# VectorE's modulation slots are loaded at their own turn, and the condition rows are made behind each FFN's first up tile

## The chip, the cores and the metric

One core of one Trainium2 chip runs the whole program in one launch. The metric is the device time in microseconds, the median of several runs of the same kernel. TensorE is PE in the views, VectorE is DVE, ScalarE is ACT, GpSimd is POOL and SyncE is SP; SP issues the large loads.

## The reference, cut to what matters

Two transformer models are chained. The first has two layers (layers 0 and 1 of the kernel) over 512 latent tokens and 256 context tokens of width 1024; the second has one layer (layer 2). Every layer is modulated by a condition vector:

```python
def adaln(cond, w_mod, b_mod):
    m = jnp.dot(jax.nn.silu(cond), w_mod) + b_mod
    return jnp.split(m[..., None, :], 6, axis=-1)

sh1, sc1, g1, sh2, sc2, g2 = adaln(c, w_mod[l], b_mod[l])
h = modulate(rms_norm(x, norm1_g[l]), sh1, sc1)
...
x = x + g1 * jnp.einsum('blm,md->bld', mix, w_out[l])
x = x + g2 * swiglu(modulate(rms_norm(x, norm2_g[l]), sh2, sc2), w_ffn_in[l], w_ffn_out[l])
```

`w_mod` is 1024 x 6144 per layer, and it meets two condition vectors (latent and context), so it is a weight that is read once for two columns. `w_out` is 1024 x 1024, the FFN's hidden width is 2816. All of it is float32.

## The kernel before, in words

**Matmuls.** Each large product is made of three fp32r matmuls (`mm3`): high part by high part, high by low, low by high. Every weight therefore passes through a preparation: SP loads halves of 512 KB (128 x 1024) into the pool `raw`, which has four buffers; ScalarE casts quarters of 128 x 512 to `whi` (L242); GpSimd subtracts to get `wlo` (L244). The pool of `whi`/`wlo` holds two weights, so the cast of a weight waits until the matmuls of the one before the last are through.

**Two queues of loads.** The class `Weights` (L215 to L252) keeps a list of loads and gives them out in order. `next` (L248) issues whatever is missing up to one entry *ahead* of the one that it gives out. There are two such objects: `W` for the weights and `WM` for the modulation. A modulation *slot* is 256 columns of `w_mod`, 1 MB; it takes two `raw` buffers and holds them until its arithmetic is done. There are 72 slots, in the order of the list `MODS`, 24 for each layer. Both objects draw from the same four buffers and the same SP queue.

**Where slots are made.** The first 20 slots, and slots 48 and 49, are made by TensorE. The other 50 (`MODS_ROWS`: slots 20 to 47 in the FFN of layer 0, slots 50 to 71 in the FFN of layer 1) are made by VectorE in `mod_rows` (L357): four instructions of 128 x 1024 for each slot, two for each half and one condition vector each (L365, results `mjunk` or `raw`), and a small addition of the bias (L373, L377). They multiply by the *condition rows* `cr`: `cond_rows` (L348) loads them from DRAM on ScalarE's queue (L352) and passes them through two Silu of 128 x 1024 on ScalarE (L354). In the kernel before, `cond_rows` is called ahead of `ffn` in each of the layers 0 and 1.

**Order of the work.** The stages of a layer are: attention, pooling and convolution mixers; the out projection (`out_proj`), of which weight slots 2 and 3 of `w_out` come behind slots 0 and 1; the norm (`norm_mod`) of each half of 256 tokens as soon as that half of `xt` is through; then `ffn`, 22 up tiles of 128 gate and 128 up columns in groups, each group followed by its down projection. In layer 1 the out projection's last part has 8 tiles for each of two halves of the latent tokens; every tile ends in a `flush` on VectorE (L936, `xt` plus gated product), and the next tile but one into the same PSUM buffer waits for it. The norm squares `xt` on ScalarE (L437), sums partly on GpSimd (L441), makes the sums over partitions on TensorE (L449), scales them on VectorE (`rsv`, L310), takes the power on GpSimd (`rsy`, L311), transposes it to rows on TensorE (L336) and then makes `u` (L464), `hh` (L467) and `hl` (L470, L472).

In `ffn` each up tile j is 16 products of three matmuls with 512 columns into `s2t` (two buffers); then ScalarE's Silu of the gate half (L996), VectorE's product `sg` (L997), the split into `gh` and `gl`, and then `mod_fill(MODS_FFN[l][j])`, which makes so many slots there. `at[j]` is a hook that is called after tile j.

The program's order is not the final order on an engine: a list scheduler places each engine's instructions by its own estimate of when they are ready, within the dependencies and buffers. A small edit can therefore shift neighbours.

Of the kernel before, what the change touches and what calls it, by code (L numbers as in the profile page):

```python
# [24 lines left out]
NJ = FF // 128  # L25
# [91 lines left out]
MODS_ROWS = set(MODS[20:48] + MODS[50:72])  # L117
# [97 lines left out]
class Weights:  # L215


    def __init__(self, k, specs, ahead=1):
        self.k, self.specs, self.ahead = k, specs, ahead
        self.done, self.used, self.q = 0, 0, []  # L220

    def _load(self, spec):
        k, nc = self.k, self.k.nc
        kind, ap, n = spec
        hn = n // 2
        halves = (slice(0, hn), slice(hn, n))
        if kind == "mod":
            raws = []
            for s in halves:
                raw = k.p_raw.tile([128, hn], F32, tag="raw", name="raw")  # L230
                nc.sync.dma_start(out=raw, in_=ap[:, s])
                raws.append(raw)
            return raws
        p = k.p_w
        hi = p.tile([128, n], F32R, tag="whi", name="whi")
        lo = p.tile([128, n], F32R, tag="wlo", name="wlo")
        for s in halves:
            raw = k.p_raw.tile([128, hn], F32, tag="raw", name="raw")
            nc.sync.dma_start(out=raw, in_=ap[:, s])
            for q in (slice(0, hn // 2), slice(hn // 2, hn)):  # L240
                h = hi[:, s][:, q]
                nc.scalar.copy(out=h, in_=raw[:, q])  # L242
                eng = nc.vector if kind == "w2" and q.start else nc.gpsimd
                eng.tensor_tensor(out=lo[:, s][:, q], in0=raw[:, q], in1=h.bitcast(F32), op=ALU.subtract)  # L244
        return hi, lo

    def next(self, key):
        while self.done < min(len(self.specs), self.used + 1 + self.ahead):  # L248
            self.q.append(self._load(self.specs[self.done][1:]))
            self.done += 1  # L250
        assert self.specs[self.used][0] == key, (self.specs[self.used][0], key)
        self.used += 1  # L252
        return self.q.pop(0)


class K:
# [492 lines left out]


    MODS_MIX = [(4, 8, 0, 0), (0, 0, 2, 0)]
    MODS_FFN = [[2 if j % 4 == 1 else 1 for j in range(NJ)], [1] * NJ, [0] * NJ]

    LAST = [(0, 0, 0.2, 0.4, 0.6, 0.8, 1), (0, 0.1, 0.4, 0.7, 1)]
    SLOT = {"g": 0, "u": 1, "p": 2, "v0": 3, "q0": 4, "q1": 5, "v1": 6, "q2": 7, "q3": 8}
# [208 lines left out]
    def ffn(self, l, pf, hx, hc, xt, xc, then, at=None):  # L964
# [5 lines left out]
        for gi, (j0, jn, cn) in enumerate(DOWN[l]):  # L970
            gt = []
            for j in range(j0, j0 + jn):
# [28 lines left out]
                gt.append((gh, gl))  # L1001
                self.mod_fill(self.MODS_FFN[l][j], "ap", j == j0 + jn - 1)
                if at and j in at:
# [31 lines left out]
    def layer(self, l, then):  # L1035
# [8 lines left out]
        with self.pool(f"a{l}") as pa, self.pool(f"b{l}") as pb:  # L1044
# [4 lines left out]
            with self.pool(f"mix{l}") as pmix:  # L1049
# [79 lines left out]
                with self.urgent(0 if full else 500):  # L1129
                    run(win[0])  # L1130
                cur, k = -1, 0
                for hd in self.attn(pa, l, qk, v, mix, lambda g: splits(g, (3,))):
                    if hd != cur:
                        run(win[cur + 1][k:] if cur >= 0 else ())
                        self.flush_items((f"q{hd}", f"v{hd // 2}"))
                        if hd == 3:
                            hm, hmc = self.new_h("x"), (self.new_h("c") if full else None)
                        cur, k, t = hd, 0, 0
                    t += 1
                    n = int(len(win[hd + 1]) * share[hd + 1][t] + 0.01)  # L1140
                    run(win[hd + 1][k:n])
                    k = n
                    self.tick(4.0)
# [460 lines left out]
    def run(self):  # L1604
        nc, tc, I = self.nc, self.tc, self.I
# [22 lines left out]
        self.cond("c", "c_ctx")  # L1628
        self.W = Weights(self, self.plan())
        self.mods = list(MODS)  # L1630
        self.WM = Weights(self, [(("mod", l, s), "mod", I[f"w_mod{l}"][s], 2048) for l, s in self.mods])
        xs = [[p_dram.tile([128, KD * 256], F32, name=f"xs{l}{i}") for i in range(2)] for l in range(2)]
        v3 = lambda ap: ap.rearrange("p (k n) -> p k n", k=KD)

# [5 lines left out]
        def store_xt(dst, xt):  # L1640
            for i in range(2):
                (nc.sync, nc.scalar)[i].dma_start(out=v3(dst[i]), in_=xt[i])

        def norm_x(l, which, xt, dst, i):
            self.norm_mod(l, which, xt[i], 0, dst, G(i), i == 1)

        def norms(l, which, xt, dst, xc=None, dstc=None):

            def f(g):
                if g == 0:  # L1650
                    self.norm_mod(l, which, xc, 1, dstc)
                else:
                    norm_x(l, which, xt, dst, g - 1)
            return f
# [27 lines left out]
        xc, xt = self.x[0], self.x[1:]  # L1682
        with self.pool("u0") as self.p_u:
            h2c, h2 = self.new_h("c"), self.new_h("x")
            self.out_proj(0, self.out_weights(0, 2, 3), hm, hmc, xt, xc, norms(0, 2, xt, h2, xc, h2c))
            self.hc, self.hx = self.new_h("c"), self.new_h("x")
            with self.pool("f0", bufs=6) as pf:
                self.cond_rows(pf, 0)
                self.ffn(0, pf, h2, h2c, xt, xc, norms(1, 1, xt, self.hx, xc, self.hc))
            store_xt(xs[0], xt)  # L1690
        xpool.close()
        if self.stop == 0:
# [2 lines left out]
        xt = self.x[1:]  # L1695
        with self.pool("u1") as self.p_u:
            h2 = self.new_h("x")
            self.out_proj(1, self.out_weights(1, 2, 3), hm, None, xt, None, norms(1, 2, xt, h2))
            self.hc, self.hx = self.new_h("c"), self.new_h("x")
            with self.pool("f1", bufs=10) as pf:  # L1700
                self.cond_rows(pf, 1)
                xc2 = self.load_x(pf, "xc2", v3(I["c2T"]), NCX, 1)
                self.ffn(1, pf, h2, None, xt, None, norms(2, 1, xt, self.hx), {13: lambda: self.norm_mod(2, 1, xc2, 1, self.hc)})
            store_xt(xs[1], xt)
        xpool.close()
        if self.stop == 1:
# [6 lines left out]
        with self.pool("mix2") as pmix:  # L1713
            hm, xt = self.block2_mix(pmix, residual2)
        with self.pool("u2") as self.p_u:
            h2 = self.new_h("x")
# [87 lines left out]
```

## Time and profile before

| | |
|---|---|
| runs | 2583.49, 2572.78, 2583.26 us; median 2583.26 us |
| the profiled execution | 2590.84 us |
| its span, first to last instruction | 2589.0 us |
| mean granted TensorE clock | 0.964 of full speed |
| PE busy | 2424.3 us, 94% of the span |
| DVE, POOL, ACT busy | 1251.9, 1192.0, 887.6 us (48%, 46%, 34%) |
| mean DMA rate | 97 GB/s |

The profiled execution is 7.6 us above the median. PE's share is so high that only stretches in which it stands still, or runs at the low clock, can give time back; the layout in time matters: layer 0's out projection ends its first part near 424 us, layer 0's FFN fills 480 to 960 us, layer 1's out projection lies at 1310 to 1360 us, its FFN's first tiles at 1360 to 1390 us, and the FFN goes on to 1740 us.

### The profile page before, as it was taken

How to read it: one execution, taken by the hardware profiler on the slowest of the kernel's cores; microseconds unless marked ns; L12 is line 12 of the kernel's file. 1: busy time of each engine (PE TensorE's matmuls, PEld its weight loads, DVE VectorE, ACT ScalarE, POOL GpSimd, SP SyncE). 2: the span in 40 equal slices, each digit the busy share in tenths (PEclk: the TensorE clock that was granted, in tenths of full speed). 3: DMA queues.
4: the chain of work that ended last, by engine and by line, in shares of the span. 5: the costliest groups of instructions: out<-in, count | busy, mean ns of one | idle time of the engine just before them, and what ended most of it. 6: DMA issues, size and time to landing. Idle time of an engine off the chain costs nothing. (4 is left out here: it accounts for less than half of the span.)

```text
span 2589.0 us, 37145 instructions
## 1 busy us (share of the span) xinstructions
PE 2424.3 (94%) x14940; PEld 2121.5 (82%) x14940; DVE 1251.9 (48%) x2247; ACT 887.6 (34%) x1863; POOL 1192.0 (46%) x960
## 2 busy tenths in 40 slices
PE   7889979999999999988978999999998899999998
PEld 5878869988888889878778787888887788888887
DVE  4897464743533464497636455364322746210113
ACT  4334453312112124333534223224443543422222
POOL 3644323634334345555327656555222353555553
PEclk8889989999999999999989999999998899999999
DMA  7213312433423332211224544443111021233221
GB/s 244 63 50 111 121 69 66 139 113 107 139 90 130 106 125 82 68 34 37 94 82 135 166 147 155 141 144 100 39 37 47 17 98 50 82 97 97 95 94 57
DMA packets 69259, 250.53 MB, mean 97 GB/s; under 512 B 7520, under 2 KB 10848, under 8 KB 67168
## 3 DMA queue, kind: packets, MB, share of 16 engines
q1 hardware_dynamic: 65568, 232.29, 27.8%
q10 hardware_dynamic: 3520, 15.88, 1.6%
q8 instruction: 117, 1.92, 0.3%
q14 instruction: 54, 0.44, 0.1%
HBM read 241.85 MB, written 6.29 MB: 96 GB/s over the span
## 5 line engine op out<-in xcount | busy, mean ns | idle before, releaser
L244 POOL TENSOR_TENSOR wlo<-raw,whi 128x512 fp32r<-128x512 f32 x564 | 782.5, 1417 | 808.7 <-ACT whi L242 808.3
L242 ACT CAST whi<-raw 128x512 fp32r<-128x512 f32 x576 | 315.9, 616 | 784.6 <-PE s2t L271 378.6
L268 PE MATMUL s2t<-hh,whi 128*128 128x512 f32 (+1 forms) x1184 | 443.3, 376 | 3.6 <-DVE sg L997 3.6
L272 PE MATMUL s2t<-hh,wlo 128*128 128x512 f32 (+1 forms) x1184 | 443.9, 375 | 2.5 <-POOL wlo L244 2.5
L271 PE MATMUL s2t<-hl,whi 128*128 128x512 f32 (+1 forms) x1184 | 444.2, 376 | 1.1 <-POOL hl L470 1.1
L268 PE MATMUL pj<-hh,whi 128*128 128x256 f32 (+1 forms) x1088 | 337.2, 312 | 9.3 <-ACT hh L467 3.2
L271 PE MATMUL pj<-hl,whi 128*128 128x256 f32 (+1 forms) x1088 | 333.5, 307 | 2.1 <-POOL hl L470 1.1
L272 PE MATMUL pj<-hh,wlo 128*128 128x256 f32 (+1 forms) x1088 | 333.3, 308 | 0.0
L268 PEld LDWEIGHTS s2t<-hh,whi 128*128 128x128 f32 x1184 | 224.9, 191 | 45.2 <-DVE sg L997 5.9
L272 PEld LDWEIGHTS s2t<-hh,wlo 128*128 128x128 f32 x1184 | 225.6, 191 | 41.7 <-POOL wlo L244 2.9
L271 PEld LDWEIGHTS s2t<-hl,whi 128*128 128x128 f32 x1184 | 225.3, 190 | 41.1 <-POOL hl L470 1.9
L268 PEld LDWEIGHTS pj<-hh,whi 128*128 128x128 f32 x1088 | 212.8, 196 | 24.4 <-ACT hh L467 4.7
L365 DVE SCALAR_TENSOR_TENSOR mjunk<-raw,cr 128x1024 f32<-128x1024 f32 x100 | 140.3, 1403 | 178.9 <-DMA raw<-in_w_mod 166.4
L271 PEld LDWEIGHTS pj<-hl,whi 128*128 128x128 f32 x1088 | 212.0, 195 | 11.7 <-POOL hl L470 1.4
L272 PEld LDWEIGHTS pj<-hh,wlo 128*128 128x128 f32 x1088 | 212.2, 195 | 8.6 <-issue 1.3
L268 PE MATMUL pj<-whi,hh 128*128 128x256 f32 x672 | 197.3, 294 | 1.3 <-ACT v L741 0.9
L997 DVE TENSOR_TENSOR sg<-sg,s2t 128x512 f32<-128x512 f32 x66 | 45.0, 683 | 314.6 <-ACT sg L996 314.6
L271 PE MATMUL pj<-wlo,hh 128*128 128x256 f32 x672 | 196.2, 292 | 0.0
L272 PE MATMUL pj<-whi,hl 128*128 128x256 f32 x672 | 194.8, 290 | 0.0
L936 DVE SCALAR_TENSOR_TENSOR xt<-pj,mod,xt 128x256 f32<-128x256 f32 x224 | 101.7, 479 | 137.3 <-PE pj L272 137.0
L365 DVE SCALAR_TENSOR_TENSOR raw<-raw,cr 128x1024 f32<-128x1024 f32 x100 | 149.7, 1497 | 5.8
L271 PE MATMUL pj<-gl,whi 128*128 128x512 f32 (+1 forms) x400 | 144.2, 361 | 0.0
(392 smaller groups left out, 4644.0 us busy)
## 6 DMA issues: line engine op xcount, KB each, us to landing
raw<-in_w_mod SPq DMA_DIRECT2D x144, 512.0 KB, 4.2
raw<-in_w_up SPq DMA_DIRECT2D x132, 512.0 KB, 3.8
raw<-in_w_dn SPq DMA_DIRECT2D x66, 512.0 KB, 3.8
raw<-in_w_in SPq DMA_DIRECT2D x60, 512.0 KB, 3.9
raw<-in_w_out SPq DMA_DIRECT2D x24, 512.0 KB, 3.8
xt<-xs ACTq DMA_DIRECT2D x4, 1024.0 KB, 6.0
xt<-in_xT ACTq DMA_DIRECT2D x2, 1024.0 KB, 8.2
cr<-in_cr ACTq DMA_DIRECT2D x2, 1024.0 KB, 4.9
```

The lines of the kernel that those rows point to most:

```text
L242: nc.scalar.copy(out=h, in_=raw[:, q])
L244: eng.tensor_tensor(out=lo[:, s][:, q], in0=raw[:, q], in1=h.bitcast(F32), op=ALU.subtract)
L268: i = mm(ps, lhsT=lh, rhs=rh, start=start, stop=False)
L271: mm(ps, lhsT=lh, rhs=rl, start=False, stop=False)
L272: return mm(ps, lhsT=ll, rhs=rh, start=False, stop=stop)
L365: nc.vector.scalar_tensor_tensor(out=raw[i] if ci else self.junk, in0=raw[i], scalar=1.0, in1=self.CR[:, ci], op0=ALU.mult, op1=ALU.mult, ...
L936: self.nc.vector.scalar_tensor_tensor(out=x, in0=ps, scalar=col, in1=x, op0=ALU.mult, op1=ALU.add)
L997: nc.vector.tensor_tensor(out=sg[:, c], in0=sg[:, c], in1=p[:, 1], op=ALU.mult)
```

## The change

The slots of `MODS_ROWS` get a kind of their own, "rows". `next` does not load such a slot ahead: only when it is the slot that is asked for. `cond_rows` is no longer called ahead of `ffn` but through the hook behind up tile 0. Since no slot can be made before the condition rows are there, the two tables of how many slots each tile makes start with 0; the slots of tile 0 are moved to later tiles. The number of slots stays 28 in layer 0 and 22 in layer 1, and no engine gets or loses an instruction.

```diff
-        if kind == "mod":
+        if kind in ("mod", "rows"):
...
     def next(self, key):
-        while self.done < min(len(self.specs), self.used + 1 + self.ahead):
+        while self.done < min(len(self.specs), self.used + 1 + self.ahead) and (self.done <= self.used or self.specs[self.done][1] != "rows"):
             self.q.append(self._load(self.specs[self.done][1:]))
...
-    MODS_FFN = [[2 if j % 4 == 1 else 1 for j in range(NJ)], [1] * NJ, [0] * NJ]
+    MODS_FFN = [[0, 2, 2, 1] + [2 if j in (5, 9, 13, 17, 20) else 1 for j in range(4, NJ)], [0, 2] + [1] * 20, [0] * NJ]
...
-        self.WM = Weights(self, [(("mod", l, s), "mod", I[f"w_mod{l}"][s], 2048) for l, s in self.mods])
+        self.WM = Weights(self, [(("mod", l, s), "rows" if (l, s) in MODS_ROWS else "mod", I[f"w_mod{l}"][s], 2048) for l, s in self.mods])
...
-                self.cond_rows(pf, 0)
-                self.ffn(0, pf, h2, h2c, xt, xc, norms(1, 1, xt, self.hx, xc, self.hc))
+                self.ffn(0, pf, h2, h2c, xt, xc, norms(1, 1, xt, self.hx, xc, self.hc), {0: lambda: self.cond_rows(pf, 0)})
...
-                self.cond_rows(pf, 1)
                 xc2 = self.load_x(pf, "xc2", v3(I["c2T"]), NCX, 1)
-                self.ffn(1, pf, h2, None, xt, None, norms(2, 1, xt, self.hx), {13: lambda: self.norm_mod(2, 1, xc2, 1, self.hc)})
+                self.ffn(1, pf, h2, None, xt, None, norms(2, 1, xt, self.hx), {0: lambda: self.cond_rows(pf, 1), 13: lambda: self.norm_mod(2, 1, xc2, 1, self.hc)})
```

The lines of the changed kernel are one higher from L216 on. What the scheduler makes of it is read from the order of each engine's instructions. First SP, the loads of layer 1's out projection and of the FFN's first up tiles (`w_out` x2 is half of a pair of weight slots, `w_mod` x2 one modulation slot); before:

```order
L239 DMA raw<-in_w_out 128x1024 x2
L231 DMA raw<-in_w_mod 128x1024 x4
L239 DMA raw<-in_w_out 128x1024 x6
L239 DMA raw<-in_w_up 128x1024 x4
L231 DMA raw<-in_w_mod 128x1024 x2
L239 DMA raw<-in_w_up 128x1024 x2
L231 DMA raw<-in_w_mod 128x1024 x2
```

and now:

```order
L240 DMA raw<-in_w_out 128x1024 x2
L232 DMA raw<-in_w_mod 128x1024 x2
L240 DMA raw<-in_w_out 128x1024 x6
L240 DMA raw<-in_w_up 128x1024 x6
L232 DMA raw<-in_w_mod 128x1024 x4
L240 DMA raw<-in_w_up 128x1024 x2
```

One slot's two loads have moved from ahead of the last six loads of `w_out` to behind the third up tile's weight; from the fourth row on the two kinds take turns as before.

Second ScalarE in the same out projection, from the casts of the last `w_out` slots to the norm's squares (`s<-xt`; `mix` and `hh` belong to the attention's last head, `xc` is a load for layer 2); before:

```order
L242 CAST whi<-raw 128x512 x4
L910 ACTIVATE mix_9866<-ap,gs_94 128x256
L340 CAST hh<-mix_9866 128x256
L352 DMA cr<-in_cr 128x2048
L1601 DMA xc_13318<-in_c2T 128x2048
L242 CAST whi<-raw 128x512 x2
L354 ACT_TABLE_LOAD
L354 ACTIVATE cr<-cr 128x1024 x2
L242 CAST whi<-raw 128x512 x2
L437 ACTIVATE s<-xt_12392 128x256 x8
```

and now:

```order
L243 CAST whi<-raw 128x512 x8
L911 ACTIVATE mix_9866<-ap,gs_94 128x256
L341 CAST hh<-mix_9866 128x256
L1602 DMA xc_13309<-in_c2T 128x2048
L353 DMA cr<-in_cr 128x2048
L438 ACTIVATE s<-xt_12388 128x256 x6
L355 ACT_TABLE_LOAD
L355 ACTIVATE cr<-cr 128x1024 x2
L438 ACTIVATE s<-xt_12388 128x256 x2
```

The eight casts stand in one piece, and the table load and the two Silu have moved from between the casts to between the squares. On VectorE the five instructions of the slot (L365 x4, L373) that stood ahead of this out projection's first flush are gone from there. In layer 0 the Silu keep their place ahead of the casts.

Third VectorE at the norm of the second half ahead of layer 1's FFN; before:

```order
L472 SCALAR_TENSOR_TENSOR hl<-u,mod_87,hh 128x256
L365 SCALAR_TENSOR_TENSOR mjunk,macc<-raw,cr 128x1024
L365 SCALAR_TENSOR_TENSOR raw,macc<-raw,cr 128x1024
L310 TENSOR_SCALAR rsv<-ap 128x1 x2
L365 SCALAR_TENSOR_TENSOR mjunk,macc<-raw,cr 128x1024
L472 SCALAR_TENSOR_TENSOR hl<-u,mod_87,hh 128x256
L365 SCALAR_TENSOR_TENSOR raw,macc<-raw,cr 128x1024
L373 TENSOR_TENSOR mod_88<-macc,PV 128x4
L377 SCALAR_TENSOR_TENSOR mod_88<-mod_88,PV 128x4
L464 SCALAR_TENSOR_TENSOR u<-xt_12394,mod_87,ap 128x256 x4
```

and now:

```order
L473 SCALAR_TENSOR_TENSOR hl<-u,mod_87,hh 128x256
L311 TENSOR_SCALAR rsv<-ap 128x1 x2
L473 SCALAR_TENSOR_TENSOR hl<-u,mod_87,hh 128x256
L366 SCALAR_TENSOR_TENSOR mjunk,macc<-raw,cr 128x1024
L465 SCALAR_TENSOR_TENSOR u<-xt_12390,mod_87,ap 128x256 x3
L366 SCALAR_TENSOR_TENSOR raw,macc<-raw,cr 128x1024
L465 SCALAR_TENSOR_TENSOR u<-xt_12390,mod_87,ap 128x256
L366 SCALAR_TENSOR_TENSOR mjunk,macc<-raw,cr 128x1024
```

The scaling `rsv` no longer stands behind two instructions of a slot; one of them now stands ahead of `u`. The scheduler also shifts neighbours elsewhere, most in layer 1's attention.

## Rows read from the trace of the kernel before

**Rows 1.** Windows: start:end, us, then PE, PEld, DVE, ACT, POOL busy (instructions), clock, DMA share, GB/s.

```profile
1320.00:1330.00 10.00, 2.43 (x12) 2.23 (x13) 0.00 (x0) 2.34 (x3) 3.15 (x4) 0.72 0.75 301
1330.00:1340.00 10.00, 4.86 (x23) 4.07 (x23) 8.57 (x13) 4.32 (x9) 5.57 (x4) 0.67 0.43 122
1340.00:1350.00 10.00, 10.00 (x68) 10.00 (x67) 2.42 (x5) 2.47 (x6) 3.33 (x5) 0.76 0.26 89
1350.00:1360.00 10.00, 10.00 (x87) 10.00 (x86) 6.11 (x15) 5.05 (x13) 2.19 (x3) 1.00 0.00 0
...
1370.00:1380.00 10.00, 5.49 (x24) 4.60 (x25) 8.21 (x15) 1.92 (x5) 9.84 (x9) 0.61 0.55 184
...
480.00:960.00 480.00, 478.04 (x2794) 423.62 (x2794) 219.76 (x395) 99.76 (x182) 200.08 (x139) 1.00 0.37 118
```

**Rows 2.** Timeline of PE, layer 1's out projection: start, duration, instruction, [idle before <-releaser].

```profile
1328.31 0.58 PE L268 MATMUL s<-hh,whi 128*128 128x256 f32 x1 [7.27 <-ACT whi L242]
...
1338.81 0.58 PE L268 MATMUL s<-hh,whi 128*128 128x256 f32 x1 [2.67 <-DVE xt L936]
```

**Rows 3.** Timeline of ACT, the same stretch.

```profile
1315.61 2.18 ACT L242 CAST whi<-raw 128x512 fp32r<-128x512 f32 x4 [2.97 <-PE pj L271]
...
1327.64 1.14 ACT L242 CAST whi<-raw 128x512 fp32r<-128x512 f32 x2 [9.03 <-DMA raw<-in_w_out]
1328.79 1.28 ACT L354 ACT_TABLE_LOAD   x1
1330.09 2.00 ACT L354 ACTIVATE cr<-cr 128x1024 f32<-128x1024 f32 x2
1332.00 1.12 ACT L242 CAST whi<-raw 128x512 fp32r<-128x512 f32 x2
```

**Rows 4.** Timeline of DVE, the same stretch.

```profile
1331.18 1.23 DVE L365 SCALAR_TENSOR_TENSOR mjunk<-raw,cr 128x1024 f32<-128x1024 f32 x1 [12.05 <-ACT cr L354]
...
1338.28 0.48 DVE L936 SCALAR_TENSOR_TENSOR xt<-s,mod,xt 128x256 f32<-128x256 f32 x1
```

**Rows 5.** Timeline of SP's DMA queue: issues, with the wait for a buffer in the duration.

```profile
1227.84 29.54 SPq L231 DMA_DIRECT2D raw<-in_w_mod  x4
...
1318.87 2.96 SPq L239 DMA_DIRECT2D raw<-in_w_out  x2
```

**Rows 6.** Waits of SP's queue, whole span: waited for, us, times, longest.

```profile
SPq L239 <- DVE raw L365: 345.1, 62, 71.0
```

**Rows 7.** Timeline of ACT, layer 0's out projection.

```profile
413.92 4.26 ACT L242 CAST whi<-raw 128x512 fp32r<-128x512 f32 x8 [11.19 <-PE pj L271]
```

**Rows 8.** Timeline of POOL, the same.

```profile
414.62 9.94 POOL L244 TENSOR_TENSOR wlo<-raw,whi 128x512 fp32r<-128x512 f32 x8 [22.34 <-ACT whi L242]
```

**Rows 9.** Timeline of PE, the same.

```profile
424.34 0.39 PE L268 MATMUL s<-hh,whi 128*128 128x256 f32 x1 [0.22 <-DVE xc L936]
```

**Rows 10.** Timeline of DVE, the norm ahead of layer 1's FFN.

```profile
1366.70 2.04 DVE L365 SCALAR_TENSOR_TENSOR mjunk<-raw,cr 128x1024 f32<-128x1024 f32 x1 [3.36 <-DMA raw<-in_w_mod]
...
1370.88 0.21 DVE L310 TENSOR_SCALAR rsv<-ap 128x1 f32<-128x1 f32 x2
```

**Rows 11.** Timeline of POOL, the same.

```profile
1366.38 7.90 POOL L244 TENSOR_TENSOR wlo<-raw,whi 128x512 fp32r<-128x512 f32 x4
...
1375.10 1.69 POOL L311 TENSOR_TENSOR rsy<-rsv,mhalf 128x2 f32<-128x2 f32 x1
```

**Rows 12.** Timeline of PE, the same.

```profile
1367.29 0.61 PE L449 MATMUL ap<-ones,s 128*128 128x128 f32 x4
...
1376.84 0.69 PE L336 MATMUL ap<-ident,rsy 128*128 128x128 f32 x2 [3.28 <-POOL rsy L311]
```

**Rows 13.** Waits of all engines, whole span: waited for, us, times, longest.

```profile
DVE mjunk L365 <- DMA raw<-in_w_mod: 166.4, 53, 7.0
```

**Rows 14.** Timeline of PE, inside layer 1's FFN.

```profile
1433.22 0.54 PE L268 MATMUL s2t<-hh,whi 128*128 128x512 f32 x1 [1.91 <-DVE sg L997]
```

**Rows 15.** The page, section 6: DMA issues, size, us to landing.

```profile
raw<-in_w_mod SPq DMA_DIRECT2D x144, 512.0 KB, 4.2
```

## The prediction

> **What bounds the kernel now.** I read the windows first, for the stretches in which TensorE (PE) is not full, then the timelines of the engines there, then the waits. PE is the bound wherever weights arrive in time: inside layer 0's FFN it is busy 478.04 of 480 us [rows 1], so nothing that the other engines do there can be worth more than 2 us. The stretch that stands out is layer 1's out projection: PE is busy 2.43 and 4.86 of 10 us in the two windows from 1320 us, then full in the third but with 68 matmuls where the fourth, at full clock, has 87, because the granted clock is 0.76 there, a mean of its levels of 1.2 and 2.4 GHz, after it fell to 0.67 in the half idle window before [rows 1]. The second such place is the entry to layer 1's FFN: 5.49 of 10 us busy, clock 0.61, from 1370 us [rows 1].
>
> Why PE stands still there can be followed through five engines. PE waits 7.27 us for a cast of `w_out`'s last slots and, at the end, 2.67 us for a flush on VectorE [rows 2]. ScalarE casts four quarters at 1315.61, and then waits 9.03 us for the load of the second half; when it has landed, two casts are made, then comes a table load and the Silu of the condition rows (1.28 and 2.00 us), and only at 1332.00 the last two casts [rows 3]. VectorE meanwhile waits 12.05 us for the condition rows, makes one modulation slot from 1331.18 on, and only then, at 1338.28, the flushes of tiles that PE had ended before [rows 4]. And the load is late because SP issues it at 1318.87: two slots' loads (x4) stand ahead of `w_out`'s last six in SP's order and were issued at 1227.84 [rows 5]. The second of these slots is the first for VectorE, is loaded one turn ahead and holds two of the four `raw` buffers until its four instructions are made after 1331 us. SP's loads of weights wait 345.1 us in all, in 62 pieces, for a slot's last instruction on VectorE [rows 6].
>
> **The change part by part.** (a) *The slot's load leaves the front of layer 1's out projection, the Silu leave the casts, and the slot's arithmetic leaves the front of the flushes.* All three meet in one stretch, so they are priced as one: by its counterpart. In layer 0 the same last slots of `w_out` are cast in one piece of eight (413.92 us, 4.26 us long) [rows 7], the eight subtractions follow in one piece of 9.94 us, which is the pace [rows 8], and PE goes on without a gap at 424.34, after four tiles [rows 9]: 424.34 - 413.92 = 10.4 us from the first cast. Layer 1's stretch takes 1338.81 - 1315.61 = 23.2 us for the same four tiles [rows 2, 3]. The order now gives layer 1 the same piece of eight casts. That is 12.8 us. The low clock behind it costs (87 - 68) x 10/87 = 2.2 us more in the window from 1340 [rows 1]; layer 0's short gaps leave no such mark in that form, so I count it: 15.0 us. Bounds: below, the wait for the load and the flush stay halfway, and only the 7.27 us of the longest gap go; above, the end is limited by casts and subtractions, which I move no further than 2 us better than layer 0's (7.3 to 17). I take 15, since the two stretches are the same code with the same sizes.
>
> The Silu and the table load, 3.3 us [rows 3], do not vanish; they now stand between the squares of the first half's norm. The cover there is the second half's eight tiles: 12 matmuls each at 10/87 us [rows 1] is 1.4 us a tile, 11 us in all. Without it the norm's squares, and with them the FFN's first matmul, would come 3.3 us later. I take 0.
>
> (b) *The FFN's entry in layer 1.* The sums over partitions of the second half end at 1367.29 + 0.61 = 1367.9 on PE [rows 12]; `rsv` comes only at 1370.88, behind two instructions of a slot that had waited 3.36 us for its load [rows 10]. GpSimd makes four subtractions beside them in 7.90 us, and `rsy` from 1375.10 on [rows 11]; PE waits 3.28 us for it, to 1376.84 [rows 12]. Four subtractions without VectorE's long instructions beside them cost half of layer 0's eight, 9.94 / 2 = 5.0 us [rows 8]. Then `rsy` can come at 1366.38 + 5.0 = 1371.4 and, even at the 1.69 us that it takes today [rows 11], end by 1373.1 instead of 1376.8: 3.7 us, and with some of the clock of 0.61 in that window [rows 1] I take 5. What is late next is `u`: it now has one slot instruction ahead of it, whose load stands behind three up tiles in SP's order. If that load holds `u` up by its full landing of 4.2 us [rows 15], the gain is eaten: bounds 0 to 8.
>
> (c) *Layer 0.* The order moves the first slot's instructions from among the flushes to the FFN's entry. There PE has the context's 256 tokens to do ahead of the second half of the latents, so I take 0; bounds: four instructions of 1.23 us [rows 4] in front of `u`, uncovered, 4.9 us later, or as much less where they stood before. The FFN behind it is full [rows 1]: 0, at best 2 us.
>
> (d) *Inside layer 1's FFN.* Slots are now loaded at their own turn, but SP's order there is the same alternation of one weight and one slot, because buffers and not the program's calls set when a load can start. VectorE already waits 166.4 us in 53 pieces for slots that were asked for one turn ahead [rows 13]. I take 0, with 4 us either way: PE loses 1.91 us to `sg` at one of these places today [rows 14].
>
> Here a rule speaks against the change. The Trainium skill ("DMA: Bandwidth & Descriptors", section "Rules for kernel authors") says to issue a DMA early and to wait for it late, so that its fixed cost overlaps with compute; by it the change gives a cover away at each of 50 slots. It is the first rival below.
>
> (e) *Layer 1's attention is reordered* by the scheduler, with no instruction more or less. No row prices that; I take 0 with 6 us either way, less than half of what (a) shows that one bad order can cost.
>
> The sum: -15 - 5 = -20 us against the profiled execution's 2590.84, that is 2570.8. That execution lies 7.6 us above the median of 2583.26, so I forecast 2583.3 - 20 = **2563 us**. Half a per cent, about what a measurement can tell from no change, is 12.9 us: faster means under 2570.3, slower over 2596.2.
>
> **The rivals.**
>
> *Slower: loads at their own turn make VectorE late for `sg`.* In layer 1 each of 20 tiles makes one slot. If the load of a slot is not there at its turn, VectorE waits up to 4.2 us for it [rows 15] with the next tile's `sg` queued behind; then come four instructions of 1.23 us = 4.9 us [rows 4] and `sg`, which I estimate at 1 us, twice a flush with half the columns [rows 4]. A tile on PE is 48 matmuls of 512 columns, as long as 96 of 256: 96 x 10/87 = 11.0 us [rows 1]. 4.2 + 4.9 + 1 = 10.1 us still fits; the rival decides from the point at which a load is over 5 us late, for instance because it also waits for a buffer that the slot before still holds. If then PE loses 1.91 us [rows 14] at each of 20 tiles, that is 38 us: 2563 + 38 = 2601. For it: VectorE's waits for loads reach 7.0 us today [rows 13]. Against it: SP's order inside the FFN hardly moves, and two `s2t` buffers let PE run a tile ahead. The rule cited above would have it this way.
>
> *The gain is only partly reached: 2571 to 2590.* Either the reordered attention costs its 6 us, or `w_out`'s last half is still late since one more buffer is held than I see, and only 7.3 us of (a) come. With 7.3 + 0 the time is 2576, with 6 us lost in attention 2582. For it: the scheduler's orders are not meant for the chip's times. Against it: the new order of ScalarE is that of layer 0.
>
> *The change doesn't do all it says.* In layer 0 the Silu keep their place ahead of the casts, so `cond_rows` is not moved there in effect; only the load's rule is. Since layer 0 has no gap to win, this changes no term; it matters only as a sign that (a) is a layer 1 effect.
>
> *More than forecast: 2540 to 2552.* (a) at 17, (b) at 8, 4 us inside the FFN and 6 us in the attention: 35 us, 2548.
>
> **How the numbers follow.** Forecast, 2552 to 2570: 0.56. Partly reached, 2571 to 2590: 0.27, with most of it under 2581. More than forecast: 0.07. Slower: 0.10. The range 2547 to 2581 holds the forecast's case, about 0.20 of the partial one and 0.04 of the larger one, together 0.80. Faster by over 0.5%: 0.56 + 0.07 = 0.63. Within: 0.27. Slower: 0.10.
>
> **What would show it.** In the profile of the changed kernel, (a) is right if ScalarE's casts of `w_out`'s last slots in layer 1 stand as one group of eight of some 4.3 us, PE's gap of 7 us behind ACT is gone, and the clock does not leave 1.00 in the three windows after it; (b) if `rsv` follows the sums within 0.5 us and PE's wait for `rsy` is under 1 us; (c) and (d) if PE in layer 0's FFN stays at 99% and PE's waits for `sg` in layer 1's FFN stay under 5 us in all. The prediction is wrong if `w_out`'s last load is still issued behind a slot's arithmetic, or if PE's waits for `sg` grow to tens of us.

## The result, and the profile after

| | before | after |
|---|---|---|
| median of the runs | 2583.38 us (2572.78 to 2587.14, 4 runs) | 2558.35 us (2556.39 to 2560.76, 4 runs) |
| ratio | | 0.9898, 95% interval 0.988 to 0.9915 |
| the profiled execution | 2590.84 us | 2556.39 us |
| its span | 2589.0 us | 2554.2 us |
| mean granted clock | 0.964 | 0.972 |
| PE busy | 2424.3 us | 2406.7 us |

The kernel became 25 us faster where 20 were forecast. A second measurement of the changed kernel, beside the last experiments, gave 2554.65 us against 2581.65, ratio 0.9893 (0.9877 to 0.9909).

The windows of the changed kernel (columns as in [rows 1]) show layer 1's out projection, which now begins at 1300.84:

```profile
480.00:960.00 480.00, 478.09 (x2770) 422.68 (x2770) 230.68 (x397) 99.30 (x180) 204.32 (x138) 1.00 0.38 119
...
1300.00:1310.00 10.00, 7.90 (x60) 7.08 (x58) 2.35 (x5) 5.04 (x10) 8.75 (x8) 1.00 0.41 125
1310.00:1320.00 10.00, 9.29 (x75) 9.08 (x76) 4.08 (x9) 5.27 (x9) 5.37 (x7) 1.00 0.78 296
1320.00:1330.00 10.00, 9.89 (x83) 9.69 (x83) 5.59 (x14) 5.78 (x16) 2.01 (x3) 1.00 0.00 0
1330.00:1340.00 10.00, 8.70 (x70) 8.08 (x69) 4.04 (x9) 9.59 (x24) 9.23 (x9) 1.00 0.37 107
1340.00:1350.00 10.00, 6.71 (x35) 6.06 (x34) 6.75 (x13) 2.92 (x7) 9.92 (x10) 0.71 0.53 156
```

The out projection ends at 1330.93. Of its windows only the first two lose anything (2.10 and 0.71 us), and the clock stays at 1.00 up to the FFN's entry (1340 us). The two half idle windows and the one at clock 0.76 of [rows 1] are gone. The FFN of layer 0 (first line) is as full as before. Why it is so stands in the timelines of ACT, of PE (those of its instructions that wait) and of SP's queue, start and duration first:

```profile
1300.84 4.26 ACT L243 CAST whi<-raw 128x512 fp32r<-128x512 f32 x8 [1.53 <-PE pj L272]
...
1315.59 1.28 ACT L355 ACT_TABLE_LOAD   x1
1318.44 2.01 ACT L355 ACTIVATE cr<-cr 128x1024 f32<-128x1024 f32 x2 [1.56 <-DMA cr<-in_cr]
```

```profile
1305.37 0.39 PE L273 MATMUL s<-hh,wlo 128*128 128x256 f32 x1 [0.80 <-POOL wlo L245]
...
1308.02 0.39 PE L273 MATMUL s<-hh,wlo 128*128 128x256 f32 x1 [0.95 <-POOL wlo L245]
...
1310.49 0.39 PE L273 MATMUL s<-hh,wlo 128*128 128x256 f32 x1 [0.78 <-POOL wlo L245]
...
1311.46 0.39 PE L269 MATMUL s<-hh,whi 128*128 128x256 f32 x1 [0.22 <-DVE xt L937]
```

```profile
1304.12 32.38 SPq L240 DMA_DIRECT2D raw<-in_w_up  x6
1339.52 12.77 SPq L232 DMA_DIRECT2D raw<-in_w_mod  x4
```

The eight casts are one piece of 4.26 us, as in [rows 7]; the table load and the Silu come 10 us behind them; PE's longest wait here is 0.95 us instead of 7.27 [rows 2]. SP has no load of `w_out` left to issue at that time: it is at the up tiles from 1304.12 on, and the first slots of VectorE come behind these, at 1339.52.

At the entry to the FFN the same views (DVE, POOL, PE) show a gain and a new wait:

```profile
1336.91 0.38 DVE L311 TENSOR_SCALAR rsv<-ap 128x1 f32<-128x1 f32 x2 [3.17 <-PE ap L450]
...
1343.25 1.22 DVE L366 SCALAR_TENSOR_TENSOR mjunk<-raw,cr 128x1024 f32<-128x1024 f32 x1 [4.89 <-DMA raw<-in_w_mod]
...
1344.40 1.26 DVE L465 SCALAR_TENSOR_TENSOR u<-xt,mod,ap 128x256 f32<-128x256 f32 x3
...
1354.24 0.47 DVE L465 SCALAR_TENSOR_TENSOR u<-xt,mod,ap 128x256 f32<-128x256 f32 x1
```

```profile
1336.78 5.20 POOL L245 TENSOR_TENSOR wlo<-raw,whi 128x512 fp32r<-128x512 f32 x4
1341.94 0.69 POOL L312 TENSOR_TENSOR rsy<-rsv,mhalf 128x2 f32<-128x2 f32 x1
```

```profile
1336.39 0.71 PE L450 MATMUL ap<-ones,s 128*128 128x128 f32 x4 [0.58 <-ACT s L438]
...
1342.69 0.43 PE L337 MATMUL ap<-ident,rsy 128*128 128x128 f32 x2 [1.04 <-POOL rsy L312]
...
1345.11 0.58 PE L272 MATMUL s2t<-hl,whi 128*128 128x256 f32 x1 [1.99 <-POOL hl L471]
```

`rsv` no longer stands behind a slot: it starts beside PE's last sums (1336.39 to 1337.10), GpSimd's four subtractions take 5.20 us instead of 7.90 [rows 11], and PE waits 1.04 us for `rsy` instead of 3.28 [rows 12]. From the end of the sums to the end of `rsy` it is 5.5 us instead of 8.9. The eight `u` behind it take longer, though. In the kernel before, the last of them is

```profile
1385.58 1.64 DVE L464 SCALAR_TENSOR_TENSOR u<-xt,mod,ap 128x256 f32<-128x256 f32 x4
```

and ends 10.4 us behind `rsy`; now the last ends 12.1 us behind it, since five instructions of slots stand in front of and between them where three stood. PE waits 1.99 us for `hl`, which is made from `u`. The 4.89 us that VectorE waits for the first slot's load are not what this costs: `u` also needs the rows that PE makes from `rsy` (L337), and these end at 1343.12, 0.13 us ahead of the slot's first instruction. The clock fell to 0.71 here.

**Where the time went.** The table cuts each profile at the same instructions of the timelines and gives the microseconds between them: start of the span to the tenth flush of `xt` out of `pj` (layer 0's mixers), to the first of the eight casts of layer 1's out projection (layer 0's FFN and layer 1's attention), to the first flush out of `s` (the four tiles of (a)), to the last flush of that out projection, to the fifth `sg` of layer 1's FFN (FFN entry), to its 22nd and last `sg` (inside FFN), to the first `sg` of layer 2's FFN (layer 2), to the end.

| kernel | layer 0 mixers | to the casts | four tiles | rest of out proj. | FFN entry | inside FFN | layer 2 | end |
|---|---|---|---|---|---|---|---|---|
| before | 406.7 | 908.9 | 22.7 | 22.8 | 84.1 | 288.6 | 497.5 | 357.7 |
| after | 398.5 | 902.4 | 10.1 | 20.0 | 82.4 | 290.8 | 492.7 | 357.4 |
| after, second profile | 401.5 | 904.2 | 10.1 | 19.6 | 82.2 | 285.9 | 491.3 | 357.4 |
| hook and table | 402.1 | 905.4 | 21.8 | 21.7 | 82.6 | 287.0 | 496.2 | 357.4 |
| rule alone | 397.3 | 906.9 | 10.1 | 19.6 | 84.7 | 290.4 | 493.0 | 357.4 |
| no Silu | 401.7 | 907.9 | 17.5 | 20.2 | 84.3 | 289.4 | 495.7 | 357.5 |
| slot 50 alone | 404.5 | 910.6 | 10.3 | 19.6 | 85.4 | 288.7 | 495.6 | 357.4 |
| slot 20 alone | 397.7 | 905.9 | 22.8 | 22.8 | 83.7 | 287.5 | 499.0 | 357.4 |
| late slots | 397.6 | 902.2 | 10.1 | 20.1 | 83.1 | 287.8 | 491.7 | 357.4 |

Two profiles of one kernel differ by up to 5 us in a stage with gaps (the second and third line), and the execution before is itself 7.5 us above its median, so only differences that many kernels share are read. The two stages of the out projection are not like that: 43.5 to 45.6 us in every kernel with the load of slot 50 ahead and the Silu between the casts, 29.7 to 31.1 in the ten profiles in which the rule holds for slot 50.

### The profile page after: what moved, and what is told of

It reads as the page before. It is cut to its first block, busy times and chain, and to the rows that moved or that the text cites. A ratio compares the mean times of both kernels' runs of the same rounds, so it can differ in the third digit from the quotient of the medians.

```text
span 2554.2 us, 37145 instructions
## 1 busy us (share of the span) xinstructions
PE 2406.7 (94%) x14940; PEld 2106.7 (82%) x14940; DVE 1243.0 (49%) x2247; ACT 888.2 (35%) x1863; POOL 1189.7 (47%) x960
## 5 line engine op out<-in xcount | busy, mean ns | idle before, releaser
L245 POOL TENSOR_TENSOR wlo<-raw,whi 128x512 fp32r<-128x512 f32 x564 | 774.3, 1403 | 762.5 <-ACT whi L243 761.9
L366 DVE SCALAR_TENSOR_TENSOR mjunk<-raw,cr 128x1024 f32<-128x1024 f32 x100 | 147.0, 1470 | 161.3 <-DMA raw<-in_w_mod 160.9
L272 PEld LDWEIGHTS pj<-hl,whi 128*128 128x128 f32 x1088 | 212.0, 195 | 12.1 <-DVE hl L473 1.9
```

The source lines that it names most:

```text
L272: mm(ps, lhsT=lh, rhs=rl, start=False, stop=False)
L366: nc.vector.scalar_tensor_tensor(out=raw[i] if ci else self.junk, in0=raw[i], scalar=1.0, in1=self.CR[:, ci], op0=ALU.mult, op1=ALU.mult, ...
```

## The experiments

The theory: a slot that is loaded ahead holds two of the four `raw` buffers, so the last loads of `w_out` come late. The rivals: it was the Silu between the casts, and the hook moves it; or only the scheduler's order changed.

**The load rule alone.** The changed kernel with the hook and the tables put back:

```diff
-    MODS_FFN = [[0, 2, 2, 1] + ..., [0, 2] + [1] * 20, [0] * NJ]
+    MODS_FFN = [[2 if j % 4 == 1 else 1 for j in range(NJ)], [1] * NJ, [0] * NJ]
...
+                self.cond_rows(pf, 1)
...
-{0: lambda: self.cond_rows(pf, 1), 13:
+{13:
```

> The load rule alone: slots for VectorE are loaded at their own turn; the condition rows are made ahead of each FFN and the tables are those of the kernel before. Theory (the slot that is loaded ahead holds two of four raw buffers): layer 1's out projection goes as in the changed kernel, from the first cast to the fifth tile in 10 to 11 us instead of 23.2, the eight casts in one piece, worth about 15 us; the entry to layer 1's FFN gains nothing or loses up to 4 us, since rsv still stands behind a slot's instruction that waits for its load. Together 2564 to 2572. Rival (the Silu between the casts and the slot's instructions ahead of the flushes are the cause, and it is the hook that moves them): the stretch stays above 20 us, 2580 or more.

Measured: 2558.42 us, ratio 0.9919 (0.9906 to 0.9932). The four tiles take 10.1 us with the condition rows still made ahead of the FFN: the rival falls. The entry gains nothing (84.7 us), since `rsv` still stands behind a slot's instruction that waits for its load. But the time is 6 us below the expected stretch: something outside the out projection gains too.

**The hook and the tables alone.** The changed kernel without the rule:

```diff
-"rows" if (l, s) in MODS_ROWS else "mod"
+"mod"
```

> The hook and the tables alone: condition rows behind up tile 0, no slot in tile 0, but slots are loaded ahead as before. Theory (buffers): w_out's last load is still issued at the slot's release, the Silu stand between the casts as before, and the out projection keeps its 23 us; only the FFN's entry gains 2 to 5 us. Together 2577 to 2584. Rival (the hook is the cause): the time of the changed kernel, 2558 to 2563.

Measured: 2575.65 us, ratio 0.9975 (0.9965 to 0.9985). ACT and PE in layer 1's out projection:

```profile
1307.52 2.18 ACT L243 CAST whi<-raw 128x512 fp32r<-128x512 f32 x4 [2.97 <-PE pj L272]
...
1318.83 1.14 ACT L243 CAST whi<-raw 128x512 fp32r<-128x512 f32 x2 [8.32 <-DMA raw<-in_w_out]
1319.98 1.28 ACT L355 ACT_TABLE_LOAD   x1
1321.28 2.00 ACT L355 ACTIVATE cr<-cr 128x1024 f32<-128x1024 f32 x2
1323.19 1.12 ACT L243 CAST whi<-raw 128x512 fp32r<-128x512 f32 x2
```

```profile
1319.50 0.58 PE L269 MATMUL s<-hh,whi 128*128 128x256 f32 x1 [6.54 <-ACT whi L243]
...
1329.80 0.58 PE L269 MATMUL s<-hh,whi 128*128 128x256 f32 x1 [2.76 <-DVE xt L937]
```

The hook is called in the program, but the scheduler puts the table load and the Silu between the casts all the same, and the casts wait 8.32 us for the late load. This is the picture of [rows 3]. The out projection still takes 43.5 us. Of the 6.8 us that it gains, 1.5 are in the entry (82.6); where the others lie, a single profile does not show.

**Rule and table, no hook.**

```diff
-..., {0: lambda: self.cond_rows(pf, 0)})
+..., )
...
+                self.cond_rows(pf, 1)
```

> The load rule and the tables, the condition rows made ahead of the FFN as in the kernel before. Theory: the hook has no part in it, so this has the time of the changed kernel, 2556 to 2562, with the Silu ahead of the squares instead of between them. Rival (the hook matters): 5 us or more above it.

Measured: 2552.98 us, ratio 0.9894 (0.9878 to 0.9909), 3 us under the stretch that was expected. The hook has no measurable part: the ratio is that of the changed kernel.

**The rule for the first slot of each FFN alone**, with hook and tables:

```diff
-"rows" if (l, s) in MODS_ROWS else "mod"
+"rows" if (l, s) in (MODS[20], MODS[50]) else "mod"
```

> The changed kernel, with the load rule for the first slot of each FFN alone; the others are loaded one ahead again. Theory (only the first slot's load lies in the out projection): the gain of 15 us there stays, and inside layer 1's FFN the 4 us that the changed kernel's profile is behind may come back: 2554 to 2559. Rival (it is loading each slot at its own turn that sets buffers free, all through the FFN): 5 us or more above the changed kernel's 2558.

Measured: 2556.48 us, ratio 0.9912 (0.9897 to 0.9927). The gain stays with two slots of fifty; loading the other 48 ahead or not cannot be told apart by this (the intervals overlap). The 4 us that might have come back inside layer 1's FFN cannot be seen either: it takes 286.8 us, between the 290.8 and 285.9 of the changed kernel's two profiles.

**The Silu left out, nothing else changed** in the kernel before:

```diff
-        for i in range(2):
-            self.nc.scalar.activation(out=self.CR[:, i], in_=self.CR[:, i], func=AF.Silu)
```

> The kernel before without the two Silu of the condition rows in either layer (they are left out, so the slots made on VectorE multiply by the plain condition). Loads and their order stay. Theory (the late load of w_out is the root): its last load is still issued when a slot is released, PE's gap for the cast stays at 7 us, and only what stood behind the Silu is saved, 3 to 8 us in the out projection: it takes 15 to 20 us from the first cast to the fifth tile. Rival (the Silu between the casts are the root): the stretch falls to 10 to 12 us and the gap of 7 us goes.

Measured: 2575.36 us, ratio 0.9968 (0.9956 to 0.9981). ACT and PE:

```profile
1309.57 2.18 ACT L242 CAST whi<-raw 128x512 fp32r<-128x512 f32 x4 [2.97 <-PE pj L271]
...
1321.52 2.21 ACT L242 CAST whi<-raw 128x512 fp32r<-128x512 f32 x4 [8.96 <-DMA raw<-in_w_out]
```

```profile
1322.19 0.58 PE L268 MATMUL s<-hh,whi 128*128 128x256 f32 x1 [7.18 <-ACT whi L242]
```

The four tiles take 17.5 us. The load is as late as before (8.96 us of waiting) and PE's gap is 7.18 us; what the Silu, with its table load and the slot that waits for it, cost on top is 22.7 - 17.5 = 5.2 us. The late load is the larger part, the Silu the smaller.

**The rule for slot 50 alone**, hook and tables as before the change:

```diff
-"rows" if (l, s) in MODS_ROWS else "mod"
+"rows" if (l, s) == MODS[50] else "mod"
```

> The kernel before, with the load rule for a single slot: slot 50, the first that VectorE makes in layer 1. Hook and tables are those of the kernel before. Theory: this one load is what the out projection of layer 1 waits for, so the stretch takes 10 to 11 us from the first cast to the fifth tile and about 15 us of the gain are there; with the shifted order of layer 1's attention and of layer 2, which came with every kernel that had the rule, 2557 to 2566. Rival (the rule works through all slots): less than 8 us of gain.

Measured: 2572.33 us, ratio 0.9957 (0.9944 to 0.9971). ACT in the out projection and DVE at the entry:

```profile
1315.18 4.27 ACT L243 CAST whi<-raw 128x512 fp32r<-128x512 f32 x8
...
1320.72 1.28 ACT L355 ACT_TABLE_LOAD   x1 [0.46 <-issue]
1327.43 2.01 ACT L355 ACTIVATE cr<-cr 128x1024 f32<-128x1024 f32 x2 [5.43 <-DMA cr<-in_cr]
```

```profile
1351.38 1.95 DVE L366 SCALAR_TENSOR_TENSOR mjunk<-raw,cr 128x1024 f32<-128x1024 f32 x1 [3.46 <-DMA raw<-in_w_mod]
...
1353.26 0.21 DVE L311 TENSOR_SCALAR rsv<-ap 128x1 f32<-128x1 f32 x2
```

The eight casts stand in one piece and the Silu behind them, though no edit touched the Silu: its place, too, followed from the load. One load of 1 MB, asked for later, takes 22.7 + 22.8 - 10.3 - 19.6 = 15.6 us out of the out projection. The whole gain is 11.9 us (2584.24 - 2572.33); of the difference 1.3 us are the longer entry, where `rsv` still waits behind a slot; the other 2.4 are too little for one profile to place. The stretch that I expected is missed from above, since I had put the shifts elsewhere into it, and they are not there.

**The rule for slot 20 alone**, the first slot of layer 0:

> The kernel before, with the load rule for slot 20 alone, the first that VectorE makes in layer 0. Layer 1's out projection keeps its early slot load. The scheduler's order of layer 0's and layer 1's attention and of layer 2 is then the shifted one of the changed kernel. Theory (the part of the gain beyond the out projection is this shift): layer 1's out projection stays at 22 to 24 us from the first cast to the fifth tile, and the shift alone gives 6 to 12 us: 2571 to 2577. Rival (the shift is worth nothing and those differences are the clock's from run to run): 2580 to 2585.

Measured: 2571.94 us, ratio 0.9966 (0.9953 to 0.998). Layer 1's out projection is that of the kernel before (22.8 and 22.8 us), and yet 9.7 us are gained. The only edit is slot 20's load, so something in or behind layer 0 gains. SP's queue changed, one row of the kernel before and one of this kernel, the last loads of layer 0's `w_out`:

```profile
331.18 77.92 SPq L239 DMA_DIRECT2D raw<-in_w_out  x4
```

```profile
325.57 3.40 SPq L240 DMA_DIRECT2D raw<-in_w_out  x2
```

In layer 0 too, a slot that was loaded ahead held buffers that `w_out` needed: four of its loads were left and the queue stood at them for 77.92 us; now two are left and they are through in 3.40. But PE did not lose that time. In the kernel before, layer 0's last casts of `w_out` waited for PE [rows 7] and not for a load, and PE's waits for the last `wlo` are 0.80 us at most there and 0.79 here.

What PE does differ in is its order. It is the same in all kernels up to one matmul in layer 0's attention, at 284.68 us before and at 280.91 here; these 3.8 us come from nothing that the edit did, for this place lies between 280.4 and 285.0 us in the fourteen profiles, with the slot ahead or not. From there to the end of the layer 0 mixers the four kernels that load slot 20 ahead take 119.6 to 122.1 us, the ten profiles that do not 116.7 to 119.6, in the mean 3.3 us less. One wait that went in all ten is this one, in the kernel before:

```profile
313.86 0.33 PE L833 MATMUL pj<-ident,y 128*128 128x128 f32 x1 [1.33 <-POOL y L812]
```

So some 3 us are in layer 0's attention and out projection, by another order. Where the other 6 of the 9.7 us lie is not shown; the interval of the ratio leaves 5 to 12 us for the whole.

The two single slots together give 11.9 + 9.7 = 21.6 us; the rule alone gives 2582.41 - 2558.42 = 24.0.

**Slots later in layer 1**, to free the entry, in the changed kernel:

```diff
-[0, 2] + [1] * 20
+[0, 0, 2, 2] + [1] * 18
```

> The changed kernel with layer 1's first slots one tile later (no slot in tiles 0 and 1, two in tiles 2 and 3). In the changed kernel VectorE waits 4.89 us for the first slot's load in front of u, and PE then waits 1.99 us for hl and runs at the low clock. Theory (the slot's load in front of u ate most of the gain at the FFN's entry): these go, 2 to 4 us less than the changed kernel, 2554 to 2556. Rival (the subtractions on GpSimd set the entry's pace anyway): no difference, 2557 to 2560.

Measured: 2552.13 us, ratio 0.9883 (0.9868 to 0.9898). VectorE at the entry:

```profile
1342.29 1.66 DVE L465 SCALAR_TENSOR_TENSOR u<-xt,mod,ap 128x256 f32<-128x256 f32 x4 [4.80 <-PE ap L337]
...
1347.41 0.47 DVE L465 SCALAR_TENSOR_TENSOR u<-xt,mod,ap 128x256 f32<-128x256 f32 x1
```

With no slot in front of `u`, VectorE waits there all the same, 4.80 us for PE's rows: the slot's load was not what held `u`. But with no slot's instruction among them the eight `u` are through 6.1 us behind `rsy` instead of 12.1, and PE's wait for `hl` falls to 0.94 us. The first `sg` comes 1355.8 - 1330.1 = 25.7 us after the out projection instead of 1363.6 - 1330.9 = 32.7, in part because only 130 matmuls of the up tiles stand ahead of it instead of 170. By the fifth `sg` all of it is lost (83.1 against 82.4 us): VectorE is full (third of the busy columns) where two tiles with two slots follow each other, and PE waits for `sg`:

```profile
1370.00:1380.00 10.00, 10.00 (x46) 8.29 (x45) 9.86 (x9) 2.78 (x5) 10.00 (x7) 1.00 0.67 218
...
1390.00:1400.00 10.00, 6.20 (x28) 4.80 (x26) 9.81 (x13) 2.55 (x5) 7.26 (x4) 1.00 0.46 133
```

```profile
1400.62 0.50 PE L269 MATMUL s2t<-hh,whi 128*128 128x512 f32 x1 [4.43 <-DVE sg L998]
```

That is the slower rival of the prediction in small: 4.43 us at one place.

The same table without the hook (rule, later table, condition rows ahead of the FFN):

> As the run before, but with the condition rows made ahead of the FFN (the load rule and the later table, no hook). Theory: the hook has no part, so the same 2 to 4 us below the run with rule and table alone, 2549 to 2552. Rival: as that run or slower, 2553 to 2558.

Measured: 2555.42 us, ratio 0.989 (0.9875 to 0.9905); not below the run without the later table, so the 2 to 4 us are not confirmed.

**Slots spread in layer 1**: `[0, 0] + [2 if j in (7, 15) else 1 for j in range(2, NJ)]`.

> The changed kernel with layer 1's slots spread: none in tiles 0 and 1, one in each later tile, and two only in tiles 7 and 15, behind which a down projection gives VectorE time. The later table of the run with two slots in tiles 2 and 3 had its entry freed, but then PE waited 4.43 us for sg, with VectorE full at 9 to 10 of 10 us. Theory (two slots in neighbouring tiles make VectorE late for sg): that wait goes and the entry stays freed, 4 to 8 us below the changed kernel: 2549 to 2554. Rival (the loads at their own turn, not the two slots, make sg late): waits for sg of some us stay, 2555 to 2560.

Measured: 2557.99 us, ratio 0.9908 (0.9895 to 0.9922): a miss. The wait of 4.43 us for `sg` is gone (1.62 at most), the FFN entry takes 77.7 us instead of 82.4, but the inside of the FFN takes 297.6 instead of 290.8. PE, behind tile 15:

```profile
1579.83 0.50 PE L272 MATMUL ap<-gl,whi 128*128 128x512 f32 x1 [2.65 <-POOL gl L342]
...
1586.59 0.50 PE L269 MATMUL ap<-gh,whi 128*128 128x512 f32 x1 [2.17 <-ACT gh L341]
```

VectorE makes the norm of layer 2's context beside tiles 13 to 15, and two slots at tile 15 make `gl` and `gh` late.

With tile 17 in place of 15:

> As the spread table before, but the second tile with two slots is 17 rather than 15. With 15, PE lost 2.65 and 2.17 us to gl and gh at the group behind tile 15, where VectorE also makes the norm of layer 2's context. Theory (a tile with two slots only costs where VectorE has other work beside it): that loss goes, the entry's gain stays, 4 to 7 us less than the spread run: 2549 to 2554, at or below the best so far. Rival (any tile with two slots costs PE some us): 2555 to 2560.

Measured: 2552.53 us, ratio 0.9887 (0.9869 to 0.9906). The entry keeps 77.4 us, the inside takes 291.7: the loss at tile 15 went. Two slots fewer are made ahead of the fifth `sg` in the two spread tables (four instead of six), so part of the entry's gain is work put off. No version clearly beats the changed kernel: the best ratios, 0.9883 and 0.9887, lie in its interval.

The changed kernel beside the last two:

> The changed kernel itself, to stand beside the two others on the same chip: 2556 to 2561. Both theories expect the same.

Measured: 2554.65 us, 1 us under the stretch that was expected.

## Why the prediction was right, point by point

(a) *Layer 1's out projection: right, mechanism and size.* 15.0 us were forecast by the counterpart in layer 0, and 22.7 + 22.8 - 10.1 - 20.0 = 15.4 came, 12.6 of them in the four tiles (forecast 12.8) and 2.8 in the rest, where 2.2 were forecast for the clock. Slot 50's rule alone does it; the hook has no part in it. The Silu behind the squares cost nothing that can be seen.

(b) *The FFN's entry: mis-sized.* 5 us were forecast, 84.1 - 82.4 = 1.7 came. The step that failed is "I take 5". Its first half held: `rsy` ends 3.4 us sooner behind the sums (3.7 forecast), and PE's wait for it, 1.04 us, just misses the sign of under 1 us. What I did not price is the slots' instructions among the eight `u`, five instead of three: they make the last `u` 1.7 us later behind `rsy`, and of the 1.3 us that I had taken for the clock nothing is seen. I named `u` as late next, but for the slot's load, and that wait of 4.89 us lies beside the wait for PE's rows. With the slots later and spread the entry takes 77.4 to 77.7 us, but with two slots fewer in it, and the whole kernel is not clearly faster for it.

(c) *Layer 0: wrong.* "I take 0" and "layer 0 has no gap to win" failed. I looked at the FFN and its entry, where it is true (478.04 and 478.09 of 480 us busy), and not at the attention ahead, which the scheduler reordered there as it did in layer 1. The run with slot 20 alone gains 9.7 us; some 3 of them are found in layer 0's attention and out projection. Whether the freed buffers could give anything there without the new order is not shown.

(d) *Inside layer 1's FFN: right.* 288.6 against 290.8 and 285.9 us. The slower rival did not come: PE's waits for `sg` grew from 3.6 us to 5.9 and 4.7 us in all there (two profiles), about the 5 us that were given as a sign. VectorE's waits for slots, over the whole span ([rows 13] before):

```profile
DVE mjunk L366 <- DMA raw<-in_w_mod: 160.9, 54, 6.6
```

166.4 us had been waited with the loads one turn ahead. The Trainium skill ("DMA: Bandwidth & Descriptors", "Rules for kernel authors") says to issue a DMA early, so that its fixed cost overlaps with compute. This case's trace shows no cover lost by the later issue (160.9 us against 166.4), and the run with the rule for two slots alone, with 48 loaded ahead, is not told apart from the changed kernel. What the early issue of slot 50 cost, buffers that a more urgent load needed, was 15.6 us.

(e) *Order of layer 1's attention: 0 taken, a gain of some us is possible, not shown.* From the tenth flush to the casts the table has 908.9 before and 902.4 and 904.2 after, of which some 1.5 lie in layer 0's FFN and its entry; the rest, 3 to 5 us, is no more than two profiles with nearly the same order differ by in this stage, as below. Layer 2, which the prediction did not mention, takes 490.5 to 493.0 us in all kernels with the rule for both first slots, and 495.6 to 499.0 in the others: some 4 us. The scheduler orders layer 2's instructions differently there. PE is busy 453.2 to 455.4 us in that stage with the rule for both and 456.3 to 459.7 without, for the same matmuls, so most of the 4 us is in the matmuls' own time and little in PE's waits; whether the new order kept the clock up or it did so for another reason stays open.

The forecast's 2563 was 4.7 us too high: -0.4 from (a), +3.3 from (b), some -3 from (c), and the rest, some -4.5, from (e) and layer 2, which the runs do not take apart.

## What to carry to other kernels

Count who holds the buffers before loading something ahead: in a pool that several streams share, a load that is early for a patient consumer is a late load for an urgent one, and the row that shows it is the queue's wait for another stream's last reader. Such a wait is a price only where the compute engine's own wait ends on that load: 7.27 us of PE's time hung on it in layer 1, and none in layer 0, where the queue stood for 77.92. Where the same code runs in two places at two speeds, the faster one prices the slower. A freed engine queue ends in the next wait, so say what then stands in front: the slots' instructions among `u`, two slots in front of `sg`. And where an engine waits for a load, ask what the next instruction would have waited for without it: here PE's rows, as long.

## What was not expected of the hardware

The changed kernel and the one with the rule for the first slots alone run nearly the same order in layer 1's attention, and PE is about as busy, but the granted clock differs. Windows of the first, then of the second:

```profile
1233.00:1243.00 10.00, 9.42 (x81) 7.77 (x80) 6.95 (x15) 5.03 (x12) 4.88 (x5) 1.00 0.11 32
1243.00:1253.00 10.00, 7.00 (x52) 4.62 (x52) 3.10 (x7) 5.64 (x13) 8.11 (x7) 1.00 0.72 236
1253.00:1263.00 10.00, 9.77 (x62) 6.88 (x60) 7.13 (x18) 6.33 (x15) 1.75 (x3) 1.00 0.12 48
```

```profile
1234.00:1244.00 10.00, 9.42 (x84) 7.96 (x82) 6.37 (x14) 5.29 (x13) 4.89 (x5) 1.00 0.05 17
1244.00:1254.00 10.00, 7.61 (x43) 5.14 (x44) 3.69 (x8) 4.82 (x10) 8.23 (x7) 0.79 0.73 247
1254.00:1264.00 10.00, 9.15 (x56) 8.09 (x55) 2.72 (x10) 2.94 (x8) 2.22 (x3) 0.69 0.15 52
```

In its window of 7.00 us busy the one stays at its high level of 2.4 GHz; in that of 7.61 the other falls, and has part of two windows at 1.2 GHz, and its stage up to the casts takes 907.3 us against 902.4. What made it fall is not shown. Executions of one kernel differ by as much (2556.39 and 2560.76 us of the changed one, at a mean granted clock of 0.972 in both), so a single profile does not tell a difference of that size.
